# Ten of the last sixteen output blocks of an encoder layer: row scale on ScalarE, addition and store on GpSimd

## The chip, the core and the metric

The kernel runs on one core of a Trainium2 chip. The metric is the device time of one execution in microseconds (us), lower is better. The core has five engines with instruction queues of their own: TensorE (PE in the profile: matmuls; PEld: its weight loads), VectorE (DVE), ScalarE (ACT), GpSimd (POOL) and SyncE (SP, which here only issues DMA transfers). Each engine takes its instructions strictly in the order of its queue and waits on semaphores for the others.

## The reference

One encoder layer over 1024 tokens of width 2048. What matters here is its end: the merged branch output is multiplied with `w_out`, each row of the product is normalised by its own root mean square, multiplied with a gain and a gate per column, and added to the input.

```python
def rmsnorm(x, g):
    xf = x.astype(jnp.float32)
    xf = xf * lax.rsqrt(jnp.mean(xf * xf, axis=-1, keepdims=True) + EPS)
    return xf.astype(x.dtype) * g
...
    merged = g_a * (y_a @ w_br_attn) + g_p * (y_p @ w_br_pool)
    o = merged @ w_out
    return x + gate[:, None] * rmsnorm(o, post_g)
```

## The kernel before

All large products are done as Strassen products of 2 x 2 blocks, seven instead of eight. Each float32 operand is split into a rounded part and a remainder (`whi`, `wlo` for weights, `mh`, `ml` for the moving operand): ScalarE writes the rounded part (L95), VectorE the remainder (L96), and three matmuls (L1194 to L1196) multiply them.

The product with `w_out` is the last stage. The 1024 rows are eight row tiles T = 0 to 7 of 128 rows; the 2048 columns are four column blocks n = 0 to 3 of 512. `out_pair(half, i, ...)` runs four times, for (0, 0), (0, 1), (1, 0), (1, 1); a half is four row tiles, and i chooses two of the four column blocks. Each call runs seven products in the order A11, S3, S2, A12, A22, S1, S4 with six PSUM banks: `bx`, `bz` and `bv`, two of each, one for each of two row tiles. Bank `bz` is used on: after S1, ScalarE copies it out (`u4`, the two L1276 instructions `u<-Z`), and S4 then adds to it. So the matmuls of S4 on a bank wait for that copy.

As each block of `o` gets ready, `result` (L1279) takes the sum of squares of its 512 columns on ScalarE (`square`, L1204: an activation and a read of its accumulator) and multiplies the block with gain and gate on VectorE (L1284). When a row tile has all four blocks, `row_scale` (L1206) makes the factor of its 128 rows: a sum on VectorE, a square root on ScalarE, a reciprocal on VectorE. Then `finish_block` (L1213) does, per block, one VectorE instruction `r * scale + x` (L1215) and a store of 256 KB, which SyncE issues, except for the blocks of the first half, whose stores GpSimd issues.

The very end is the call (1, 1), `final`. Before its last product, S4, the blocks of T = 4 and 5 are complete: `after()`, which is `third_block` (L1415), finishes these eight. Then S4 runs 24 matmuls for the bank of T = 6, block 1 of that row tile gets ready, and its four blocks are finished; then 24 matmuls for T = 7 and the same again. The eight weight pieces of S4 have buffers of their own, and their splitting on ScalarE and VectorE (the last `whi` and `wlo`) stands in the queues around the finishing blocks. The order within each queue comes from a scheduler that places instructions by its own estimate; `keep` marks an instruction that is to stay in program order. The rows of `x` for T = 4 to 7 (`xr`) were loaded during earlier products.

Of the kernel before, what the change touches and what calls it, by code (L numbers as in the profile page):

```python
# [14 lines left out]
AF = mybir.ActivationFunctionType  # L15
ALU = mybir.AluOpType
# [26 lines left out]
def encoder_layer(ctx: ExitStack, tc: tile.TileContext, x, c, table, w_ada, b_ada, pre_g,  # L43
# [15 lines left out]
    nc = tc.nc  # L59
# [30 lines left out]
    def keep(ins):  # L90

        tc.keep_in_program_order(ins)
# [259 lines left out]
    for r0, src in ((0, c[0]), (16, b_ada[0, 0:D]), (32, b_ada[0, D:2 * D]),  # L352
                    (48, pre_g[0]), (64, b_merge[0]), (96, pool_scale[0])):
        n = src.shape[0] // P
# [421 lines left out]
    held = {}  # L776
# [414 lines left out]
    def out_mm(pb, op, name, j, t, w, first, last):  # L1191
        ts_ = slice(t * P, (t + 1) * P)
        hi, lo = (o_[:, j % 2, ts_] for o_ in op[name][j // 2])
        nc.tensor.matmul(pb, hi, w[0], start=first, stop=False, skip_group_check=True)  # L1194
        nc.tensor.matmul(pb, lo, w[0], start=False, stop=False, skip_group_check=True)  # L1195
        nc.tensor.matmul(pb, hi, w[1], start=False, stop=last, skip_group_check=True)  # L1196

    xrow, held = {}, {}

    def rows_of(T, n):  # L1200
        return out[T * P:(T + 1) * P, n * 512:(n + 1) * 512]
# [4 lines left out]
    def row_scale(T):  # L1206
        s_ = const.tile([P, 3], F32, tag="st", name=uid("st"), bufs=4)
        nc.vector.tensor_reduce(s_[:, 0:1], ssq[:, T], op=ALU.add, axis=AX.X)
        nc.scalar.activation(s_[:, 1:2], s_[:, 0:1], AF.Sqrt, bias=eps_t, scale=1.0 / D)
        nc.vector.reciprocal(s_[:, 2:3], s_[:, 1:2])  # L1210
        return s_[:, 2:3]

    def finish_block(T, n, scale, store=store):  # L1213
        r = held.pop((T, n))
        keep(nc.vector.scalar_tensor_tensor(r, r, scale, xrow.pop((T, n)), op0=ALU.mult, op1=ALU.add))  # L1215
        store(rows_of(T, n), r)

    def fetch_x_block(T, n, tile_of):
        xrow[T, n] = tile_of("xr")
        load(xrow[T, n], x[T * P:(T + 1) * P, n * 512:(n + 1) * 512])  # L1220
# [7 lines left out]
    def out_pair(half, i, op, between, after=None):  # L1228
# [50 lines left out]
        def result(blk, t, src, dst):  # L1279

            T, nh = half * 4 + (int(blk[1]) - 1) * 2 + t, int(blk[0]) - 1
            n = 2 * nh + i
            square(src, T, n)
            nc.vector.tensor_tensor(dst, src, g[nh], ALU.mult)  # L1284
            if stays:
                held[T, n] = dst
            else:
                nc.gpsimd.dma_start(o_d[T * P:(T + 1) * P, n * 512:(n + 1) * 512], dst)
# [41 lines left out]
        for t in range(2):  # L1330
            for j, w in enumerate(ws):
                out_mm(bz[t], op, "B22", j, t, w, False, j == len(ws) - 1)
            result("12", t, bz[t], c12[t])
            scale = row_scale(6 + t)
            for n in (0, 2, 3, 1):
                finish_block(6 + t, n, scale)

    nextm, nextt2 = [], {}
    scales = {}
# [4 lines left out]
    def first_rows(T, n):  # L1344

        def place(name):
            ring.rotate(-1)
            return ring[-1]

        def fetch():  # L1350
            if (T, n) not in held:
                held[T, n] = place("fo")
                keep(load(held[T, n], o_d[T * P:(T + 1) * P, n * 512:(n + 1) * 512]))
            fetch_x_block(T, n, place)

        def put_out():
            if T not in scales:
                scales[T] = row_scale(T)
            finish_block(T, n, scales[T], nc.gpsimd.dma_start)

        return fetch, put_out
# [45 lines left out]
    def between_11(n, jp):  # L1407
        if jp % 2 and n < 3:
            steps(1)
        if jp == JP - 1 and n in (2, 4):  # L1410
            for T in (4, 5) if n == 2 else (6, 7):
                for b in range(4):
                    fetch_x_block(T, b, lambda name: slot(name, F32))

    def third_block():  # L1415
        assert not side
        for T in (4, 5):
            scale = row_scale(T)
            for b in range(4):
                finish_block(T, b, scale)  # L1420

    out_pair(0, 0, ops[0], between_00)
    out_pair(0, 1, ops[0], between_01)
    out_pair(1, 0, ops[1], between_10)
    out_pair(1, 1, ops[1], between_11, third_block)


# [36 lines left out]
```

## Time and profile before

| | us |
|---|---|
| median of 3 runs | 2125.08 (2124.27 to 2125.27) |
| profiled execution, its own time | 2122.46 |
| span of its profile | 2120.7 |
| PE busy | 2089.0 (99%) |
| DVE busy | 1538.7 (73%) |
| ACT busy | 1109.5 (52%) |
| POOL busy | 20.4 (1%), 90 instructions |

The span runs from the first to the last recorded event of the execution; its own time is 1.8 us longer. The profile numbers times from the start of the span. "Busy" counts the time in which an engine had an instruction under way, and successive instructions of an engine overlap: four `whi` splits recorded with about 0.6 us each take 2.23 us together. So what one more instruction costs its queue is the distance from start to start, not the recorded length. DMA issues are not counted as busy. Landing is the time from an issue to the arrival of the last byte.

### The profile page before, as it was taken

Reading aid. Unit: us, or ns where it says so; the run is one execution under the profiler, and the core shown is the slowest. Engines: PE = TensorE matmul, PEld = TensorE weight load, DVE = VectorE, ACT = ScalarE, POOL = GpSimd, SP = SyncE. Lnnn points to the kernel's source line nnn. Section 1 sums busy time; section 2 is a strip of 40 time slices with the busy share of each in tenths; the row PEclk is TensorE's granted clock in tenths of the full one; section 3 lists DMA queues with packets and bytes.
Section 4 is the critical chain, followed back from the end, with each engine's and each line's share of the span. In section 5 each row is a group of like instructions: output and inputs, shape, how many; then the busy total and the mean of one; then the engine's idle time right before and its main releaser. Section 6 shows DMA issues by size and latency. Waiting matters only on the chain.

```text
span 2120.7 us, 28959 instructions
## 1 busy us (share of the span) xinstructions
PE 2089.0 (99%) x9567; PEld 1715.1 (81%) x9567; DVE 1538.7 (73%) x2754; ACT 1109.5 (52%) x2102; POOL 20.4 (1%) x90
## 2 busy tenths in 40 slices
PE   6999999999999999999999999999999999999998
PEld 4588888888888888888888888888788788888886
DVE  5786667777547676677777678856957977889667
ACT  5654444444474544666665544333645644767654
POOL 0000000000000000000000000000000000000000
PEclk9999999999999999999999999999999999999999
DMA  9886566899676356544645477676754556686996
GB/s 330 271 269 216 187 208 219 307 310 316 223 228 210 120 176 204 174 157 159 196 149 162 154 236 235 206 221 195 237 173 160 187 194 198 218 311 216 296 342 221
DMA packets 301718, 466.10 MB, mean 220 GB/s; under 512 B 23882, under 2 KB 144866, under 8 KB 301568
## 3 DMA queue, kind: packets, MB, share of 16 engines
q1 hardware_dynamic: 298192, 455.72, 65.9%
q0 software_dynamic: 3040, 8.48, 1.1%
q8 instruction: 75, 1.23, 0.2%
q14 instruction: 75, 0.61, 0.1%
q10 hardware_dynamic: 336, 0.06, 0.0%
HBM read 340.41 MB, written 125.85 MB: 220 GB/s over the span
## 4 chain that ended last, share of the span: by engine, by line
PE 90%; DVE 5%; DMA 3%; issue 1%; ACT 1%; SPq 0%; ACTq 0%; DVEq 0%
PE Z L235 30%; PE X L235 20%; PE V L235 20%; PE Z L1194 2%; PE Z L1195 2%; PE Z L1196 2%; PE V L1196 1%; PE X L1196 1%; PE X L1195 1%; PE V L1195 1%; PE V L1194 1%; PE X L1194 1%; PE GEMV L455 1%; DMA raw<-in_w_merge_dram 1%; DVE wlo L96 1%; PE PT L905 1%
## 5 line engine op out<-in xcount | busy, mean ns | idle before, releaser
L95 ACT ACTIVATE whi<-raw 128x512 fp32r<-128x512 f32 (+1 forms) x528 | 321.8, 610 | 526.1 <-PE Z L235 260.4
L96 DVE TENSOR_TENSOR wlo<-raw,whi 128x512 fp32r<-128x512 f32 (+1 forms) x528 | 347.0, 661 | 166.7 <-PE Z L235 129.8
L96 DVE TENSOR_TENSOR wlo<-wr,whi 128x512 fp32r<-128x512 f32 x224 | 151.0, 688 | 55.9 <-ACT whi L95 49.8
L95 ACT ACTIVATE whi<-wr 128x512 fp32r<-128x512 f32 x224 | 138.8, 629 | 89.7 <-DVE wlo L96 37.2
L102 DVE TENSOR_TENSOR raw<-raw,raw 128x512 f32<-128x512 f32 x80 | 55.2, 690 | 105.0 <-DMA raw<-in_w_merge_dram 77.2
L235 PE MATMUL V<-T3h,whi 128*128 128x512 f32 x336 | 92.0, 393 | 0.6 <-DVE u L102 0.6
L235 PE MATMUL X<-B11h,whi 128*128 128x512 f32 x336 | 92.0, 392 | 0.0
L95 ACT ACTIVATE whi<-ws 128x512 fp32r<-128x512 f32 (+1 forms) x88 | 53.7, 611 | 73.0 <-PE X L235 67.7
L235 PE MATMUL V<-T4l,whi 128*128 128x512 f32 x336 | 91.2, 390 | 0.7 <-DVE T4l L96 0.6
L235 PE MATMUL Z<-T1h,whi 128*128 128x512 f32 x336 | 91.6, 391 | 0.0
L235 PE MATMUL Z<-T2h,whi 128*128 128x512 f32 x336 | 91.5, 392 | 0.1
L235 PE MATMUL Z<-B22h,whi 128*128 128x512 f32 x336 | 91.5, 392 | 0.0
L235 PE MATMUL Z<-T2h,wlo 128*128 128x512 f32 x336 | 90.8, 390 | 0.5 <-DVE wlo L96 0.5
L235 PE MATMUL X<-B21h,whi 128*128 128x512 f32 x336 | 91.2, 391 | 0.0
L235 PE MATMUL V<-T4h,whi 128*128 128x512 f32 x336 | 91.2, 391 | 0.0
L235 PE MATMUL Z<-T1l,whi 128*128 128x512 f32 x336 | 91.0, 390 | 0.1
L235 PE MATMUL X<-B11l,whi 128*128 128x512 f32 x336 | 90.9, 390 | 0.0
L235 PE MATMUL X<-B11h,wlo 128*128 128x512 f32 x336 | 90.7, 390 | 0.0
L235 PE MATMUL Z<-B22l,whi 128*128 128x512 f32 x336 | 90.7, 390 | 0.0
L235 PE MATMUL V<-T3l,whi 128*128 128x512 f32 x336 | 90.7, 390 | 0.0
L235 PE MATMUL Z<-T1h,wlo 128*128 128x512 f32 x336 | 90.6, 390 | 0.0
L235 PE MATMUL X<-B21l,whi 128*128 128x512 f32 x336 | 90.6, 389 | 0.0
(315 smaller groups left out, 4819.3 us busy)
## 6 DMA issues: line engine op xcount, KB each, us to landing
part<-part_d SPq DMA_DIRECT2D x136, 256.0 KB, 4.8
ada<-in_w_ada_dram SPq DMA_DIRECT2D x128, 256.0 KB, 5.3
raw<-in_w_in_dram SPq DMA_DIRECT2D x64, 512.0 KB, 4.1
raw<-in_w_merge_dram SPq DMA_DIRECT2D x64, 512.0 KB, 5.8
wr<-ws_dS SPq DMA_DIRECT2D x64, 512.0 KB, 5.2
wr<-in_w_out_dram SPq DMA_DIRECT2D x48, 512.0 KB, 5.4
proj_d<-part SPq DMA_DIRECT2D x68, 256.0 KB, 2.2
sw<-in_w_out_dram SPq DMA_DIRECT2D x64, 256.0 KB, 5.7
```

The source lines that it names most:

```text
L95: ins = (nc.scalar.activation(hi, src, AF.Copy), nc.vector.tensor_tensor(lo, src, f32(hi), ALU.subtract))
L96: nc.vector.tensor_tensor(lo, src, f32(hi), ALU.subtract))
L102: return (eng or nc.vector).tensor_tensor(o, a, b, ALU.add)
L235: nc.tensor.matmul(ps, w_[:, i], op[mov][j][m_], start=fresh and i == 0 and n == 0, stop=i == nj - 1 and n == 2, skip_group_check=True)
L455: ins = nc.tensor.matmul(pv[g:g + 32, :], scz[:, kc, :], tile_of(kc), start=kc < 4, stop=kc >= 12, tile_position=(0, g))
L905: nc.tensor.transpose(pt[:, i * P:(i + 1) * P], p[:, i * P:(i + 1) * P], ident)
L1194: nc.tensor.matmul(pb, hi, w[0], start=first, stop=False, skip_group_check=True)
L1195: nc.tensor.matmul(pb, lo, w[0], start=False, stop=False, skip_group_check=True)
L1196: nc.tensor.matmul(pb, hi, w[1], start=False, stop=last, skip_group_check=True)
```

## The change

`finish_aside` is a second way to finish a block: ScalarE multiplies the block with the row scale (a Copy activation with a scale for each partition), GpSimd adds x, and GpSimd issues the store. All eight blocks of T = 4 and 5 take it, and block 0 of T = 6 and of T = 7. The other six blocks of T = 6 and 7 keep the VectorE instruction and the SyncE store.

```diff
+    def finish_aside(T, n, scale):
+        r = held.pop((T, n))
+        keep(nc.scalar.activation(r, r, AF.Copy, scale=scale))
+        keep(nc.gpsimd.tensor_tensor(r, r, xrow.pop((T, n)), ALU.add))
+        nc.gpsimd.dma_start(rows_of(T, n), r)
...
             for n in (0, 2, 3, 1):
-                finish_block(6 + t, n, scale)
+                (finish_aside if n == 0 else finish_block)(6 + t, n, scale)
...
             for b in range(4):
-                finish_block(T, b, scale)
+                finish_aside(T, b, scale)
```

Lines behind L1216 move down by six: L1276 and L1284 of before are L1282 and L1290 of the changed kernel.

ScalarE's queue, from the splitting of the last weight pieces (`whi`) to the two copies `u<-Z` that free the banks for S4. Before:

```order
L95 ACTIVATE whi_19955<-wr_19949 128x512
L95 ACTIVATE whi_19961<-wr_19959 128x512
L95 ACTIVATE whi_19965<-wr_19959 128x512
L1276 ACTIVATE u_4231_19969<-Z_19341 128x512
L1276 ACTIVATE u_4232_19970<-Z_19342 128x512
L95 ACTIVATE whi_19975<-wr_19973 128x512
```

And of the changed kernel, where `mo`, `c` and `u` with `st` are the blocks of T = 4 and their scale:

```order
L95 ACTIVATE whi_19955<-wr_19949 128x512
L1220 ACTIVATE mo_19009<-mo_19009,st_19991 128x512
L95 ACTIVATE whi_19961<-wr_19959 128x512
L1220 ACTIVATE c_4162_19731<-c_4162_19731,st_19991 128x512
L95 ACTIVATE whi_19965<-wr_19959 128x512
L1220 ACTIVATE mo_18912<-mo_18912,st_19991 128x512
L1282 ACTIVATE u_4231_19969<-Z_19341 128x512
L1220 ACTIVATE u_4140_19639<-u_4140_19639,st_19991 128x512
L1282 ACTIVATE u_4232_19970<-Z_19342 128x512
L95 ACTIVATE whi_19975<-wr_19973 128x512
```

Three scalings now stand ahead of the first copy `u<-Z` and a fourth ahead of the second. The four scalings of T = 5 stand further down, ahead of the square of T = 6.

VectorE's queue, from the last weight remainder (`wlo`) to the first finishing instruction of T = 6. Before:

```order
L96 TENSOR_TENSOR wlo_19980<-wr_19973,whi_19979 128x512
L1284 TENSOR_TENSOR p_4111_19532<-p_4111_19532,pg_19435 128x512
L1215 TENSOR_SCALAR u_4140_19639<-u_4140_19639,st_19991,xr_19629 128x512
L1215 TENSOR_SCALAR mo_19009<-mo_19009,st_20003,xr_19631 128x512
L1215 TENSOR_SCALAR c_4163_19732<-c_4163_19732,st_20003,xr_19633 128x512
L1215 TENSOR_SCALAR mo_18912<-mo_18912,st_20003,xr_19635 128x512
L1215 TENSOR_SCALAR u_4141_19640<-u_4141_19640,st_20003,xr_19637 128x512
L1284 TENSOR_TENSOR c_4242_20015<-Z_19341,pg_19433 128x512
L1208 TENSOR_REDUCE st_20044<-ssq_o 128x1
L1210 RECIPROCAL st_20044<-st_20044 128x1
L1215 TENSOR_SCALAR mo_19332<-mo_19332,st_20044,xr_19827 128x512
```

And of the changed kernel:

```order
L96 TENSOR_TENSOR wlo_19980<-wr_19973,whi_19979 128x512
L1290 TENSOR_TENSOR p_4111_19532<-p_4111_19532,pg_19435 128x512
L1290 TENSOR_TENSOR c_4242_20023<-Z_19341,pg_19433 128x512
L1208 TENSOR_REDUCE st_20052<-ssq_o 128x1
L1210 RECIPROCAL st_20052<-st_20052 128x1
L1215 TENSOR_SCALAR mo_18807<-mo_18807,st_20052,xr_19831 128x512
```

The finishing instructions of T = 4 and 5 are gone (three more of them stood further up, between weight remainders), and T = 6 has three instead of four; T = 7 likewise.

GpSimd's queue, whose last entries before were the stores of the first half. The changed kernel goes on behind them (the first of ten such pairs; those of T = 6 and 7 come last):

```order
L1216 DMA out_dram<-mo_18696 128x512
L1221 TENSOR_TENSOR mo_19009<-mo_19009,xr_19623 128x512
L1222 DMA out_dram<-mo_19009 128x512
L1221 TENSOR_TENSOR c_4162_19731<-c_4162_19731,xr_19625 128x512
L1222 DMA out_dram<-c_4162_19731 128x512
L1221 TENSOR_TENSOR mo_18912<-mo_18912,xr_19627 128x512
L1222 DMA out_dram<-mo_18912 128x512
```

Each store waits for the addition ahead of it, and each addition for a scaling on ScalarE. All ten pairs stand in one queue. SyncE's queue loses the ten stores and keeps six.

## Prediction

> **What bounds the kernel now.** The page first: PE is busy over the whole span except its two ends.
>
> ```profile
> span 2120.7 us, 28959 instructions
> PE   6999999999999999999999999999999999999998
> ```
>
> Nothing before the last product moves, so only the last 25 us count. I read the timeline of each engine there, beginning with PE and ACT around the copies that free the banks.
>
> ```profile
> 2100.78 0.50 PE L1194 MATMUL Z<-whi,mh 128*128 128x512 f32 x1
> ...
> 2111.57 0.39 PE L1196 MATMUL Z<-wlo,mh 128*128 128x512 f32 x1
> ...
> 2100.78 0.19 PEld L1194 LDWEIGHTS Z<-whi,mh 128*128 128x128 f32 x1 [0.35 <-ACT u L1276]
> ```
>
> ```profile
> 2094.48 2.23 ACT L95 ACTIVATE whi<-wr 128x512 fp32r<-128x512 f32 x4
> 2097.59 0.62 ACT L95 ACTIVATE whi<-wr 128x512 fp32r<-128x512 f32 x1
> 2099.09 1.15 ACT L95 ACTIVATE whi<-wr 128x512 fp32r<-128x512 f32 x2 [0.88 <-DMA wr<-ws_dS]
> 2100.15 0.58 ACT L1276 ACTIVATE u<-Z 128x512 f32<-128x512 f32 x1
> ...
> 2112.05 0.58 ACT L1204 ACTIVATE junk<-Z 128x512 f32<-128x512 f32 x1 [1.71 <-PE Z L1196]
> 2112.54 0.19 ACT L1204 ACTIVATION_READ_ACCUMULATOR junk<-Z 128x1 f32 x1
> 2114.01 0.29 ACT L1209 ACTIVATE st<-st,eps_t 128x1 f32<-128x1 f32 x1 [1.27 <-DVE st L1208]
> ```
>
> S4 cannot start until `u<-Z` has run: PE stands still for 0.35 us and starts at 2100.78, 0.63 after the copy's start. From there its 48 matmuls run without a gap; the last starts at 2111.57 and ends at 2111.96. The copy itself starts as soon as ACT has done the splits ahead of it. So ACT's queue up to 2100.15 is on the path, with 0.88 us of slack ahead of 2099.09 (it waits for a load there) and none behind.
>
> Then the end, in the chain of waits (start, length, what) and SP's last issue.
>
> ```profile
> 2112.65 0.66 DVE c L1215
> 2113.31 0.60 DVE c L1284
> 2113.91 0.07 DVE st L1208
> 2113.99 0.02 issue
> 2114.01 0.30 ACT st L1209
> 2114.32 0.02 issue
> 2114.34 0.17 DVE st L1210
> 2114.51 0.03 issue
> 2114.54 0.75 DVE mo L1215
> ...
> 2116.61 0.66 DVE c L1215
> ```
>
> ```profile
> 2113.23 0.68 DVE L1284 TENSOR_TENSOR c<-Z,pg 128x512 f32<-128x512 f32 x1
> 2116.53 0.74 DVE L1215 SCALAR_TENSOR_TENSOR c<-c,st,xr 128x512 f32<-128x512 f32 x1
> 2117.30 0.33 SPq L1216 DMA_DIRECT2D out_dram<-c  x1
> ```
>
> VectorE is behind: its gain multiply of T = 7 (L1284) could start when the square's accumulator is read, 2112.54 + 0.19 = 2112.73, and starts at 2113.23, because finishing blocks of T = 6 stand ahead. Then come sum, root, reciprocal, four finishing instructions 0.66 apart, and the last store.
>
> ```profile
> out_dram<-mo SPq DMA_DIRECT2D x8, 256.0 KB, 2.4
> out_dram<-mo POOLq DMA_DIRECT2D x1, 256.0 KB, 3.6
> DMA to landing us min/median/max: 3.6/5.7/7.6
> ```
>
> A store by SP in this stretch lands in 2.4 us (first row, median of eight from 2095 to 2121): 2117.30 + 2.4 = 2119.7, and the span ends 1.0 us later. GpSimd's eight `mo` stores from 2015 to 2062, where loads were dense, took 3.6 to 7.6 us (third row); the 3.6 is the second row, one store at 2021.
>
> **The change part by part.**
>
> *ScalarE and the banks.* From the four splits of 2.23 us, less one length of 0.62, three distances are 1.61, so one ACT instruction of this size takes 0.54 us of the queue. The first scaling fits into the 0.88 us gap: the reciprocals that it needs end at about 2098.57. The second and third stand between the splits and ahead of the first copy, where nothing idles: 2 x 0.54 = 1.08, with a few hundredths for the first, **1.1 us**. The copy starts at 2101.25 and PE at 2101.88. The fourth scaling delays only the second copy, needed 24 matmuls later. The last weight pieces come later too, but by the same 1.1 us or less, since VectorE has lost the finishing instructions between them. So PE ends at 2111.96 + 1.1 = 2113.06. Bounds: 0.6, if a scaling takes half that distance, to 1.7, if a third fails to fit the gap.
>
> *VectorE.* Ten finishing instructions go. Those of T = 4 and 5 buy only what VectorE was late by, 2113.23 - 2112.73 = 0.50; of T = 7's four one goes, 0.66. So the SP side ends at +1.1 - 0.50 - 0.66 = **-0.1 us**: the same as before. Whatever GpSimd does, the time can hardly fall.
>
> *GpSimd, one addition.* The trace has no addition on POOL. The nearest rows:
>
> ```profile
> L1452 POOL MEMSET const-float32-0.0<- 128x1 f32 x1 | 0.1, 98 | 0.2 <-issue 0.2
> masks.py:197 POOL MEMSET ident<- 128x128 f32 x1 | 0.2, 204 | 0.3 <-POOLq L1452 0.3
> masks.py:199 POOL TENSOR_SCALAR_AFFINE_SELECT ident<-ident 128x128 f32<-128x128 f32 x1 | 0.3, 282 | 0.0
> ```
>
> A write alone costs (204 - 98) / 127 = 0.83 ns an element, a read and a write (282 - 98) / 127 = 1.45, so a read 0.62. Two reads and a write are 2.07 ns, for 512 elements with the fixed 98 ns **1.16 us**. Bounds: 0.84 (as with one input) and 1.58 (each input at the full 1.45).
>
> *GpSimd, one store.* The closest two issues in its queue stand 0.66 apart:
>
> ```profile
> 1969.61 0.54 POOL L1216 DMA_DIRECT2D out_dram<-u  x1 [3.25 <-DVE u L1215]
> 1970.27 0.54 POOL L1216 DMA_DIRECT2D out_dram<-c  x1
> ```
>
> With 0.10 for the wait between addition and store (an estimate from the 0.12 between these two rows), a block costs 1.16 + 0.10 + 0.66 = 1.92 us of POOL's queue, if nothing disturbs it. The first scaling ends near 2099.2, T = 5's follow by 2107, and POOL never runs dry. So the tenth addition starts at 2099.2 + 9 x 1.92 = 2116.5, though its own scaling is done by 2115.75 (the T = 7 chain above, 1.1 - 0.50 later, plus 0.62). It is the **backlog** that decides. Its store is issued at 2116.5 + 1.26 = 2117.7. For landing I take 3.6, the row with the lightest traffic and the nearest to the quiet end; bounds 2.4 (as SP's) and 5.7. With 1.0 to the end: 2122.3, **+1.6**.
>
> [...]
>
> *GpSimd beside VectorE.* From 2099 to 2117 VectorE still runs 15 instructions with two inputs in SBUF: five `wlo`, four on `p`, six finishing.
>
> ```profile
> L96 DVE TENSOR_TENSOR wlo<-wr,whi 128x512 fp32r<-128x512 f32 x5 | 3.4, 682 | 0.0
> L1284 DVE TENSOR_TENSOR p<-p,pg 128x512 f32<-128x512 f32 x2 | 1.4, 682 | 0.0
> L102 DVE TENSOR_TENSOR p<-p,u 128x512 f32<-128x512 f32 x2 | 1.3, 682 | 0.0
> ```
>
> Nine at 0.60 and six at 0.66 from start to start are 9.4 us. Additions fill 1.16 / 1.92 = 60% of POOL's queue, so 5.7 us of VectorE's work falls beside one. Whether they slow each other no row shows; POOL's store issues keep at 0.54 beside a VectorE busy most of the time, but they read no tile. Bounds: nothing, and the whole 5.7. I take half, **2.8 us**, about 0.3 per block, because two-input work on both sides is just what the trace has not had.
>
> **Sum.** 2120.7 + 1.6 + 2.8 = 2125.1, +4.4. The profiled execution took 2122.46, 2.6 below the median of the runs; I move the median by the same: 2125.08 + 4.4 = **2129.5 us**.
>
> **The rivals.**
>
> *POOL undisturbed.* No slowing: +1.6, 2126.7. For it: 0.54 for every store. Against it: those rows are no additions.
>
> *POOL locked out.* An addition and a two-input VectorE instruction exclude each other, and VectorE goes first: the whole 5.7, +7.3; with an addition at 1.4, halfway to the upper bound, ten times 0.24 more, +9.7. Middle 2133.6. [...]
>
> *Not slower.* The addition costs 0.84, as with one input, so a block takes 1.60 and the tenth addition starts when its scaling ends, 2115.8; and its store lands in 2.4 as SP's do: 2115.8 + 0.94 + 2.4 + 1.0 = 2120.1, so SP's side ends last at -0.1: 2125.0. It decides below 1.84 us a block and about 2.9 us of landing, together. Against it: both are at their bounds.
>
> *The relief does not come.* VectorE or PE is stalled by weight pieces split late on top of the rest: +6 or more.
>
> **How the numbers follow.** Chances: forecast 0.40 (+2.7 to +6.5), undisturbed 0.27, locked out 0.22, not slower 0.06, last 0.05. What a measurement of this kernel can tell from no change is 0.2%, 4.25 us. Above it: a bit more than half of the forecast's 0.40, and 0.22 and 0.05, together 0.52. Faster by that much would need a sum that none of these gives: 0.02. Within: 0.46. The range runs from 2125.5, under the undisturbed case, to 2135.5, past the locked-out one.
>
> **What would show it.** In the changed kernel's profile: PE's wait for `u<-Z` grown from 0.35 to about 1.4 us and its last matmul near 2112.7; VectorE idle between T = 6 and T = 7, and its last finishing instruction near 2116.5; ten POOL pairs from 2099 without idle time, 1.9 to 2.4 us apart, ending near 2121; the last landing POOL's and no longer SP's. I am wrong if POOL sits idle ahead of its last addition, if its additions are far from 1.2 to 1.5 us from start to issue, or if a PE gap other than that one opens.

## The result: 9 us slower, and the profile after

The changed kernel takes 2132.68 us (median of six runs, 2131.26 to 2133.74), the kernel before 2123.49 in six runs (2122.42 to 2125.27): a ratio of 1.0042, 95% interval 1.0031 to 1.0053, so 9 us slower. The profiled execution took 2131.3 us with a span of 2129.5, 8.8 above the span before.

TensorE first, since it set the time before: the timeline of PE in the changed kernel (start, length, operation; in brackets the idle time ahead and its releaser), from the last matmul of S1.

```profile
2099.66 0.39 PE L1196 MATMUL Z<-wlo,mh 128*128 128x512 f32 x1
2100.81 0.50 PE L1194 MATMUL Z<-whi,mh 128*128 128x512 f32 x1 [0.76 <-ACT u L1282]
...
2105.27 0.39 PE L1195 MATMUL Z<-whi,ml 128*128 128x512 f32 x1
2106.65 0.50 PE L1196 MATMUL Z<-wlo,mh 128*128 128x512 f32 x1 [0.99 <-DVE wlo L96]
...
2107.21 0.40 PE L1195 MATMUL Z<-whi,ml 128*128 128x512 f32 x1
2110.95 0.79 PE L1196 MATMUL Z<-wlo,mh 128*128 128x512 f32 x1 [3.34 <-DVE wlo L96]
2111.54 0.63 PE L1194 MATMUL Z<-whi,mh 128*128 128x512 f32 x1
2111.97 0.63 PE L1195 MATMUL Z<-whi,ml 128*128 128x512 f32 x1
...
2119.09 0.39 PE L1196 MATMUL Z<-wlo,mh 128*128 128x512 f32 x1
```

In the kernel before, that last matmul of S1 stands here:

```profile
2100.46 0.39 PE L1196 MATMUL Z<-wlo,mh 128*128 128x512 f32 x1
```

The stage that ran without a gap before now stops twice, both times for a weight remainder (`wlo`) that VectorE has not written, and behind the second stop the matmuls start 0.43 us apart instead of 0.23. The windows show the same (length, busy time and count of PE, PEld, DVE, ACT and POOL, then the granted TensorE clock, DMA share, GB/s):

```profile
2106.20:2109.60 3.40, 0.96 (x3) 0.48 (x3) 3.40 (x3) 1.43 (x3) 2.93 (x4) 1.00 0.20 77
2109.60:2116.40 6.80, 5.45 (x13) 4.29 (x14) 6.41 (x7) 1.70 (x4) 5.85 (x7) 0.50 0.36 135
2116.40:2119.80 3.40, 3.08 (x14) 2.18 (x12) 1.66 (x2) 0.23 (x1) 0.99 (x2) 1.00 0.77 288
```

From 2109.6 to 2116.4, TensorE was granted half its clock (0.50); full clock (1.00) stands on both sides.

Why the remainders are late shows where VectorE and GpSimd are laid side by side. VectorE's timeline:

```profile
2100.79 3.63 DVE L102 TENSOR_TENSOR p<-p,u 128x512 f32<-128x512 f32 x2 [0.26 <-ACT u L1282]
2104.35 2.25 DVE L96 TENSOR_TENSOR wlo<-wr,whi 128x512 fp32r<-128x512 f32 x1
...
2108.67 2.22 DVE L96 TENSOR_TENSOR wlo<-wr,whi 128x512 fp32r<-128x512 f32 x1
2110.82 2.24 DVE L1290 TENSOR_TENSOR p<-p,pg 128x512 f32<-128x512 f32 x1
2112.98 0.68 DVE L1290 TENSOR_TENSOR c<-Z,pg 128x512 f32<-128x512 f32 x1
...
2120.29 0.69 DVE L1290 TENSOR_TENSOR c<-Z,pg 128x512 f32<-128x512 f32 x1 [2.24 <-ACT junk L1204]
...
2122.94 1.75 DVE L1215 SCALAR_TENSOR_TENSOR c<-c,st,xr 128x512 f32<-128x512 f32 x1
```

And GpSimd's:

```profile
2098.09 1.29 POOL L1221 TENSOR_TENSOR mo<-mo,xr 128x512 f32<-128x512 f32 x1 [44.14 <-ACT mo L1220]
...
2104.74 1.29 POOL L1221 TENSOR_TENSOR u<-u,xr 128x512 f32<-128x512 f32 x1
...
2106.91 1.28 POOL L1221 TENSOR_TENSOR mo<-mo,xr 128x512 f32<-128x512 f32 x1
...
2115.54 1.29 POOL L1221 TENSOR_TENSOR mo<-mo,xr 128x512 f32<-128x512 f32 x1
...
2122.42 1.72 POOL L1221 TENSOR_TENSOR mo<-mo,xr 128x512 f32<-128x512 f32 x1 [4.73 <-ACT mo L1220]
```

Before the change, a VectorE instruction with two inputs in SBUF took 0.68 us, and the next one started 0.60 after it:

```profile
2104.15 0.68 DVE L1284 TENSOR_TENSOR p<-p,pg 128x512 f32<-128x512 f32 x1
2104.75 0.68 DVE L96 TENSOR_TENSOR wlo<-wr,whi 128x512 fp32r<-128x512 f32 x1
```

Now six of them, from 2100.79 to 2112.98, take 12.2 us from start to start, 2.03 each instead of 0.60. Each ends about 0.56 us after the addition beside it: the addition at 2104.74 ends at 2106.03, the remainder at 2106.60. So VectorE gets through one instruction per pair of addition and store (2.17 us). The product with one input in PSUM (`c<-Z`, 2112.98) keeps its 0.68, but it runs mostly beside a store issue, so the trials below decide about it. The additions stay at 1.27 to 1.31, one at 1.42. VectorE loses all of it, GpSimd next to nothing, except at the very end, where the tenth addition and VectorE's last instruction slow each other (1.72 for 1.29, and 1.75 for 0.74).

GpSimd is idle for 4.73 us ahead of its tenth addition, so its backlog does not set the end. The chain of waits hides that: it follows POOL's queue back, and that time stands in it as 4.93 us of "issue" from 2117.44.

The 8.8 us by stages, from the starts of matmuls here and in the timeline of before: up to the last S1 matmul **-0.80** (2099.66 for 2100.46; 0.7 of it is there when the product with `w_out` begins, 1827.5 for 1828.2, far ahead of the change, so this is scatter between executions); bank copy **+0.83** (S4's first matmul 1.15 behind that, for 0.32); S4 from first to last matmul **+7.49** (18.28 for 10.79); from the last matmul to the end of the span **+1.28** (10.41 for 9.13). S4's share is the first stop, 1.38 - 0.23 = 1.15, the second, 3.74 - 0.23 = 3.51, and the lower clock: the 13 intervals from 2110.95 to 2116.55 take 5.60 rather than 2.95, 2.65 more; 0.2 remain.

### The profile page after: what moved, and what is told of

It is laid out like the page before. It is cut to its first block, busy times and chain, and to the rows that moved or that the text cites. A ratio compares the mean times of both kernels' runs of the same rounds, so it can differ in the third digit from the quotient of the medians.

```text
span 2129.5 us, 28982 instructions
## 1 busy us (share of the span) xinstructions
PE 2092.7 (98%) x9567; PEld 1716.8 (81%) x9567; DVE 1545.2 (73%) x2744; ACT 1115.2 (52%) x2112; POOL 39.5 (2%) x110
## 4 chain that ended last, share of the span: by engine, by line
PE 91%; DVE 3%; DMA 2%; issue 1%; POOL 1%; SPq 0%; ACT 0%; ACTq 0%; POOLq 0%; DVEq 0%
PE Z L235 30%; PE V L235 20%; PE X L235 20%; PE Z L1194 2%; PE Z L1195 2%; PE Z L1196 2%; PE V L1194 1%; PE X L1194 1%; PE V L1195 1%; PE X L1195 1%; PE X L1196 1%; PE V L1196 1%; PE GEMV L455 1%; PE PT L905 1%; PE XT L407 1%
```

## The experiments

Three parts of the change could make the remainders late: the additions (theory A: an addition on GpSimd keeps VectorE's two-input instructions out), the scalings (theory B: ScalarE writes `whi` later), the store issues (theory C). The first four runs take them apart, on one chip, with 25 runs of the kernel before (median 2123.19).

**The scaling alone.** ScalarE scales, VectorE adds, SyncE stores:

```diff
+        keep(nc.scalar.activation(r, r, AF.Copy, scale=scale))
+        keep(nc.vector.tensor_tensor(r, r, xrow.pop((T, n)), ALU.add))
+        store(rows_of(T, n), r)
```

> The scalings stay on ScalarE in the changed kernel's order; the additions go to VectorE and the stores to SyncE. Theory A (a GpSimd addition keeps two-input VectorE work out while it runs, so the last weight remainders come late, PE waits and its clock drops): the wait at the bank copy stays at about 1.2 us (0.8 more than before), the two waits for wlo (1.4 and 3.8 us) vanish, the clock stays at 1.00, and the time is +0.3 to +1.0 us against before. Theory B (eight scalings in ScalarE's queue make the weight pieces late): the waits for wlo stay at 3 us or more and the time at +5 us or more.

Measured: 2125.42, ratio 1.0008 (0.9999 to 1.0017): 2.2 us by the medians, more than I expected, but not clear of no change. PE waits for the bank copy, 1.1 us, and for no remainder; VectorE's instructions keep 0.68, the last remainder among them:

```profile
2106.75 0.68 DVE L96 TENSOR_TENSOR wlo<-wr,whi 128x512 fp32r<-128x512 f32 x1
```

All ten scalings stand in ScalarE's queue, and the remainders are in time: theory B falls.

**The store alone.** VectorE's one instruction as before, GpSimd issues the ten stores:

```diff
+        keep(nc.vector.scalar_tensor_tensor(r, r, scale, xrow.pop((T, n)), op0=ALU.mult, op1=ALU.add))
+        nc.gpsimd.dma_start(rows_of(T, n), r)
```

> All finishing work on VectorE as before; only the ten stores are issued by GpSimd. Theory A: nothing is locked, VectorE's instructions keep 0.66 and 0.74 us, PE has only its 0.35 us wait, and the time is 0 to +1 us, since the last landing is still one of SyncE's. Theory C (GpSimd's store issues disturb VectorE): VectorE instructions beside the issues stretch beyond 1 us and the time is +4 us or more.

Measured: 2124.28, ratio 1.0004 (0.9995 to 1.0013). The issues take 0.54 us, and VectorE's instructions beside them 0.69 and 0.75 (GpSimd, then VectorE):

```profile
2102.50 0.54 POOL L1221 DMA_DIRECT2D out_dram<-mo  x1 [45.31 <-DVE mo L1220]
2102.72 0.75 DVE L1220 SCALAR_TENSOR_TENSOR c<-c,st,xr 128x512 f32<-128x512 f32 x1
```

Theory C falls: the issues by themselves hold nothing up. PE's wait for the bank copy was not the 0.35 that I expected but 0.89, with no scaling in ScalarE's queue: ScalarE waits 0.92 us for the load of a weight piece ahead of the copy.

**The addition with SyncE's store.**

```diff
-        nc.gpsimd.dma_start(rows_of(T, n), r)
+        store(rows_of(T, n), r)
```

> Scaling on ScalarE and addition on GpSimd as in the changed kernel, but SyncE stores. Theory A: the gaps that GpSimd's store issues leave between additions (0.87 us) shrink to 0.3 us or less while scalings are at hand, so VectorE is kept out for the four additions of T = 4 together and again for those of T = 5; the waits of PE for wlo stay, 3 to 6 us in sum, and the time is +5 to +10 us. The additions of T = 4 and 5 end by about 2112 instead of 2115. Theory C: without the store issues no VectorE instruction stretches, and the time is +1 us or less.

Measured: 2128.19, ratio 1.0023 (1.0014 to 1.0033). Scalings and additions together, without a store issue between the additions, give about half of the loss, 5.0 us, and 2.8 more than the scalings alone. The timeline of VectorE there, and then GpSimd's:

```profile
2107.26 0.68 DVE L96 TENSOR_TENSOR wlo<-wr,whi 128x512 fp32r<-128x512 f32 x1
...
2115.41 1.75 DVE L1215 SCALAR_TENSOR_TENSOR c<-c,st,xr 128x512 f32<-128x512 f32 x1
2117.08 0.68 DVE L1290 TENSOR_TENSOR c<-Z,pg 128x512 f32<-128x512 f32 x1
```

```profile
2103.34 1.75 POOL L1221 TENSOR_TENSOR mo<-mo,xr 128x512 f32<-128x512 f32 x1
2105.04 1.75 POOL L1221 TENSOR_TENSOR u<-u,xr 128x512 f32<-128x512 f32 x1
2108.79 1.50 POOL L1221 TENSOR_TENSOR mo<-mo,xr 128x512 f32<-128x512 f32 x1 [2.00 <-DMA out_dram<-u]
```

The two engines take turns, one instruction of each per 1.70 us, and both pay. The waits for remainders are smaller than expected (weight loads 0.41 and 0.67 late, PE's idle time 0.24 in all, clock at 1.00): from 2106.8 to 2108.8 GpSimd is idle (the profile names a transfer as the releaser, but the scaling that the next addition needs ends only at 2108.71), and the last two remainders (2107.26 and 2108.47) start in that pause. More is lost behind S4: T = 7's gain multiply starts at 2117.08, because T = 6's finishing instructions ahead of it are stretched. That the additions cost is confirmed; my size for the waits was not.

**One input on GpSimd.** Scaling and store as in the change, but GpSimd multiplies the block by 1.0 in place of the addition of x:

```diff
-        keep(nc.gpsimd.tensor_tensor(r, r, xrow.pop((T, n)), ALU.add))
+        keep(nc.gpsimd.tensor_scalar(r, r, 1.0, None, op0=ALU.mult))
```

> As the changed kernel, but GpSimd multiplies the block by 1.0 in place of the addition, so the ten blocks leave out x. If any GpSimd instruction that reads SBUF locks out two-input VectorE work: VectorE instructions beside it stretch to 0.7 plus its length (0.8 to 0.9 us), PE waits for wlo 0.5 to 3 us in sum, and the time is +2 to +6 us. If only GpSimd's second input does it: no stretch, only the longer bank wait, and the time is 0 to +1.5 us.

Measured: 2133.32, ratio 1.0048 (1.0033 to 1.0063), as slow as the change, for another reason. VectorE's two-input instructions take 0.68 to 1.10, one at the very end 1.30, and PE waits for no remainder; S4 starts 2.10 us behind the last matmul of S1 and goes on without a stop. But the multiplication with one input (1.50 us) is longer than the addition with two (1.27 to 1.31 in the change), as GpSimd's timeline shows:

```profile
2126.03 1.50 POOL L1222 TENSOR_SCALAR mo<-mo 128x512 f32<-128x512 f32 x1
```

Ten pairs, all but one 2.43 us apart, without idle time from 2103.71 on, in a run in which the first scaling also came late: here it is the backlog that decides. The time alone would have read as "the second input does not matter"; the views say that it does.

**Side by side, by itself.** Behind the end of the kernel before, five trials on scratch tiles, in each five instructions of VectorE or ScalarE against five of GpSimd:

```diff
+    both_sides(lambda: nc.vector.tensor_tensor(z[2], z[2], z[3], ALU.add), pool_two)
+    both_sides(lambda: nc.vector.tensor_tensor(z[2], zp, z[3], ALU.add), pool_two)
+    both_sides(lambda: nc.vector.tensor_scalar(z[2], z[2], 0.5, None, op0=ALU.mult), pool_two)
+    both_sides(lambda: nc.scalar.activation(z[2], z[2], AF.Copy), pool_two)
+    both_sides(lambda: nc.vector.tensor_tensor(z[2], z[2], z[3], ALU.add), pool_one)
```

> The kernel before with five short trials at its end on scratch tiles, 128x512 each: five instructions on GpSimd beside five on another engine. (1) GpSimd additions beside VectorE additions of two SBUF inputs: theory A wants both stretched, a VectorE one to 1.7 to 2.2 us and one per addition. (2) beside VectorE additions with one input in PSUM, (3) beside VectorE multiplications of one SBUF input, (4) beside ScalarE copies: theory A in its narrow form (only a second SBUF input of VectorE collides) wants 0.6 to 0.8 us in all three; in its wide form (any VectorE instruction is kept out) (2) and (3) stretch to 1.5 us or more. (5) one-input GpSimd multiplications beside VectorE additions of two SBUF inputs: 0.7 to 1.1 us on VectorE, as in the run with one input.

The groups of that stretch (busy time, mean ns of one, idle time; `zp` lies in PSUM, all else in SBUF):

```profile
L1443 POOL TENSOR_TENSOR z<-z,z 128x512 f32<-128x512 f32 x20 | 27.3, 1367 | 66.5 <-DVE z L1430 65.0
L1446 POOL TENSOR_SCALAR z<-z 128x512 f32<-128x512 f32 x5 | 8.3, 1656 | 0.4
L1448 DVE TENSOR_TENSOR z<-z,z 128x512 f32<-128x512 f32 x5 | 7.2, 1442 | 0.1
L1450 DVE TENSOR_SCALAR z<-z 128x512 f32<-128x512 f32 x5 | 5.9, 1180 | 0.4 <-POOL z L1440 0.3
L1452 DVE TENSOR_TENSOR z<-z,z 128x512 f32<-128x512 f32 x5 | 4.0, 807 | 0.4 <-POOL z L1440 0.3
L1449 DVE TENSOR_TENSOR z<-zp,z 128x512 f32<-128x512 f32 x5 | 3.5, 691 | 0.4 <-POOL z L1440 0.3
L1451 ACT ACTIVATE z<-z 128x512 f32<-128x512 f32 x5 | 3.1, 630 | 25.6 <-POOL z L1440 25.5
```

L1448 is the case of the change: both inputs in SBUF beside additions, 1442 ns in the mean (the first, ahead of any addition, 682; the median 1632). GpSimd's five additions there take 8.21 us from first start to last end, for 6.63 beside L1449, so both engines pay. With one input of VectorE's addition in PSUM (L1449) it is 691: for an addition, it is the second SBUF input that counts. But a VectorE multiplication with a single SBUF input (L1450) is held up too, though its first took 427: median 1368, between what the two forms of the theory wanted. No run here shows why. ScalarE (L1451) shows no delay: its five take 629 to 631 ns each, 3.28 us together, and eight such copies without GpSimd, in the run with a late piece below, 5.27, so 0.66 from start to start in both. Beside a GpSimd instruction with one input (L1452) VectorE loses little, 807 in the mean, and GpSimd is the one that goes up, to 1656 in the mean, for the 1.50 us above. So theory A holds, and for more than two-input work: of what was tried, what goes free beside an addition is VectorE reading one of its inputs from PSUM, and ScalarE.

**All scalings behind the last remainder.** The change, with the scales of T = 4 and 5 made from a read of the last remainder, so that no addition can start beside one:

```diff
+            first = row_scale(T)
+            nc.vector.scalar_tensor_tensor(scale, f32(last_lo)[:, 0:1], 0.0, first, op0=ALU.mult, op1=ALU.add)
```

> As the changed kernel, with the scalings of T = 4 and 5 held behind the last weight remainder by the same tiny instruction. Theory A: PE has no wait for wlo and its clock stays at 1.00; what then decides is GpSimd's queue: ten pairs 2.16 us apart from about 2105.6, the tenth addition starts near 2125 without idle time ahead of it, and the time is +8 to +11 us. If the queue did not matter, the time would be within +2 us.

Measured: 2135.56 beside 2122.29, ratio 1.0063 (1.0046 to 1.0080), some 13 us slower and 2 more than the upper end of what I expected. The same ten additions, later: PE stops for no remainder, S4 takes 10.77 from first to last matmul, the clock stays at 1.00. The price is the queue of GpSimd, and the finishing of T = 6 (VectorE, then GpSimd):

```profile
2113.66 2.21 DVE L1215 SCALAR_TENSOR_TENSOR mo<-mo,st,xr 128x512 f32<-128x512 f32 x1
...
2120.09 0.68 DVE L1290 TENSOR_TENSOR c<-Z,pg 128x512 f32<-128x512 f32 x1
```

```profile
2107.49 1.29 POOL L1221 TENSOR_TENSOR mo<-mo,xr 128x512 f32<-128x512 f32 x1 [51.35 <-ACT mo L1220]
...
2126.94 1.27 POOL L1221 TENSOR_TENSOR mo<-mo,xr 128x512 f32<-128x512 f32 x1
```

From 2107.49 to 2126.94 GpSimd never idles, 2.16 us a pair, and the backlog decides. Here, where the additions start nine microseconds later than in the change, the backlog is what the prediction took it for.

**Half of them, behind.** T = 4 on VectorE as before; T = 5 aside, behind the last remainder; block 0 of T = 6 and 7 aside:

```diff
+            if T == 4:
+                for b in range(4):
+                    finish_block(T, b, first)
+                continue
```

> The four blocks of T = 4 are back on VectorE, those of T = 5 and block 0 of T = 6 and 7 go aside, and the scalings of T = 5 take their scale through a tiny VectorE instruction that also reads the last weight remainder, so that no addition starts before it is done. Theory A: no wait of PE for wlo, the bank wait as before, clock 1.00; GpSimd's six pairs, 2.2 us apart from about 2106.5, end near 2119, and VectorE's finishing instructions of T = 6 and 7 stretch to 1.3 to 2.2 us beside the additions: the time is +1.5 to +4 us. If the remainders were late for another reason than the additions, the waits for wlo stay above 2 us and the time is +5 us or more.

Measured: 2128.72 beside 2122.29, ratio 1.0028 (1.0018 to 1.0038), 6 us slower where I expected at most 4. PE waits for no remainder, but six additions are enough to hold up T = 6's finishing instructions on VectorE:

```profile
2114.13 1.81 DVE L1215 SCALAR_TENSOR_TENSOR p<-p,st,xr 128x512 f32<-128x512 f32 x1
2115.86 2.23 DVE L1215 SCALAR_TENSOR_TENSOR c<-c,st,xr 128x512 f32<-128x512 f32 x1
2118.02 0.68 DVE L1290 TENSOR_TENSOR c<-Z,pg 128x512 f32<-128x512 f32 x1
```

T = 7's gain multiply could start at 2114.85, when its square's accumulator is read, and starts 3.2 us later. The hold-up moves to the next place with two-input work.

**The clock: a late piece in the kernel before.** Is the half clock a consequence of PE's stop, or of what GpSimd and VectorE do there? Ten ScalarE copies of the last S4 weight piece onto itself, ahead of its rounding:

```diff
+                if not ring and jp == JP - 1:
+                    for _ in range(10):
+                        keep(nc.scalar.activation(raw[:, 1], raw[:, 1], AF.Copy))
```

> The kernel before, with ten Copy activations of the last weight piece onto itself ahead of its split, about 5.4 us of ScalarE; GpSimd does nothing at the end. The last two weight pieces are then ready about 4 us late, so PE stands still for 3.5 to 4.5 us in one go. If PE's clock falls after any such stop: the granted clock reads 0.5 for about 5 us behind it, matmuls start 0.43 us apart instead of 0.23, and some 2.5 us are lost on top of the stop. If the fall came from GpSimd's or VectorE's state in the changed kernel: the clock stays at 1.00 and only the stop is lost.

Measured: 2125.27 beside 2122.29, clock at 1.00. Not a test: the scheduler put matmuls of T = 7 ahead of the late piece, and PE stopped for about 1.1 us only. So the run was repeated with eight and with fourteen copies, and the 48 matmuls of S4 held in their order:

```diff
-                    for _ in range(10):
+                    for _ in range(8):
...
-                out_mm(bz[t], op, "B22", j, t, w, False, j == len(ws) - 1)
+                out_mm(bz[t], op, "B22", j, t, w, False, j == len(ws) - 1, keep)
```

> The kernel before, with eight ScalarE copies of the last S4 weight piece onto itself ahead of its rounding, and S4's 48 matmuls held in the order that the kernel before has, so that TensorE meets the late piece in one stop; nothing of the change is in it. From the copies' 0.66 us start to start and the first S4 matmul at 2100.72 in the run with ten unpinned copies, the stop should be one of about 3.6 us, as long as the second one of the changed kernel (3.74 between two matmuls). If such a stop alone lowers the clock: matmuls behind it 0.43 apart for about 5 us, PEclk near 0.5 in that window, S4 from first to last matmul about 10.8 + 3.5 + 2.5 = 16.8 us. Rival, the slow matmuls of the changed kernel come from something that GpSimd or VectorE do there: matmuls stay 0.23 apart, PEclk 1.00, S4 about 14.3 us.

> As the run with eight copies, with fourteen: one stop of about 7.6 us. If a stop alone lowers the clock, it does so here too, matmuls 0.43 apart behind it for about 5 us (about 2.5 us on top of the stop), and if the shorter stop of the other run did not lower it, the threshold lies between the two. Rival: clock stays 1.00 and S4 takes about 10.8 + 7.4 = 18.2 us from first to last matmul; then what lowered the clock in the changed kernel lies in GpSimd's or VectorE's work.

Measured: 2130.63 and 2137.25 beside 2122.70, one execution each. Both traces are already 2 to 3 us behind that of before when the product with `w_out` begins near 1830, far ahead of the copies, so I read S4 alone. PE with eight copies, from the stop to the last matmul, and its windows:

```profile
2107.69 0.39 PE L1196 MATMUL Z<-wlo,mh 128*128 128x512 f32 x1
2111.62 0.50 PE L1194 MATMUL Z<-whi,mh 128*128 128x512 f32 x1 [3.54 <-ACT whi L95]
...
2120.21 0.39 PE L1196 MATMUL Z<-wlo,mh 128*128 128x512 f32 x1
```

```profile
2109.60:2113.00 3.40, 1.38 (x5) 0.83 (x6) 2.13 (x4) 2.42 (x5) 0.00 (x0) 1.00 0.65 231
2113.00:2116.40 3.40, 3.40 (x10) 2.67 (x9) 1.33 (x4) 0.98 (x3) 0.00 (x0) 0.50 0.00 0
2116.40:2119.80 3.40, 3.40 (x17) 2.80 (x16) 2.34 (x4) 0.00 (x0) 0.00 (x0) 1.00 0.67 240
```

And the windows with fourteen:

```profile
2109.70:2113.10 3.40, 0.00 (x0) 0.00 (x0) 2.47 (x4) 3.24 (x6) 0.00 (x0) 1.00 0.68 252
2113.10:2123.30 10.20, 5.98 (x14) 4.73 (x15) 3.19 (x7) 5.51 (x11) 0.00 (x0) 0.50 0.07 25
```

GpSimd does nothing there, and VectorE's instructions are those of the kernel before, at their old lengths: the stop brings the half clock without them. With eight copies, S4 takes 2120.21 - 2103.82 = 16.39 us from first to last matmul, expected 16.8: 10.79 of before, 3.70 for the stop, 1.90 for the restart and the clock (1.60 in the nine intervals at half clock). With fourteen it takes 22.00, 8.23 of it for the stop and 2.98 for the clock. The half clock (0.50) lasted 3.4 us with eight copies, 6.8 in the changed kernel and 10.2 with fourteen. In the 3.40 us ahead of it PE was busy for 1.38 us with eight copies, for 0.96 in the changed kernel and for none with fourteen. What sets its length, and the delay from the stop to its start, no run here shows.

No variant with additions on GpSimd was faster than the kernel before, and the two without them (scaling alone, store alone) cannot be told from it.

## Why the prediction was right, and where it failed

The direction was right and the time lay inside the range, but the change was twice the forecast: +9.2 by the medians, against +4.4. The forecast reached its sign by a wrong step, and that the time lay in the range is luck in good part: the backlog that the sum rests on did not set the end, and 7.3 us of two stops and a lower clock, which the sum does not have, came in its place.

- **Bank copy.** Forecast +1.1, and the two traces differ by 0.83. That looks like the term, but it is not shown to be: from the last matmul of S1 to the first of S4 it is 1.15 to 2.10 us in the four traces with scalings ahead of the copy, and 0.23 to 1.38 in those without, where a late load of a weight piece held ScalarE as well (0.92 us with the store alone). The trace of before, with 0.32, is at the low end.
- **One addition.** Estimated at 1.16 us from the fill and the select at the program's start, measured 1.27 to 1.29. Addition and store, with the 0.30 that the store waits behind the addition, take 2.17 us of the queue; forecast 1.92 undisturbed.
- **Landing of GpSimd's stores.** Taken as 3.6 us from a row in a stretch dense with loads, measured 2.6, as this row of the transfers from 2095 on shows (the last number is the median landing):

```profile
out_dram<-mo POOLq DMA_DIRECT2D x6, 256.0 KB, 2.6
```

- **The backlog.** "POOL never runs dry", so that it decides. It did run dry, for 4.73 us ahead of its last addition, because T = 7 had become so late that the backlog was gone by then. That was one sign that I had named for being wrong; a gap of PE other than the one for `u<-Z` was another, and it came too.
- **GpSimd beside VectorE: the step that failed.** The prediction had 5.7 us of VectorE's work beside additions, took half of it as a slowing, and put that on GpSimd's queue; the sharpest rival, too, had VectorE go first. In the run GpSimd kept its 1.29 us and VectorE was held: six instructions, 12.2 us for 3.6, 8.6 lost. The sentence that fell with it is that the last weight pieces come later "by the same 1.1 us or less, since VectorE has lost the finishing instructions between them". The instructions were gone, but those that stayed took three times as long, two remainders came late, and PE stopped for 1.15 and 3.51 us.
- **The clock.** 2.65 us were not in any of the cases. A stop of PE was priced at its own length only.
- **The rivals.** "Locked out" had the exclusion that the runs then showed (a VectorE addition of 0.68 us took 1.63 beside additions), with the wrong engine as its loser. "The relief does not come" (+6 or more, chance 0.05) is what happened: PE stalled by late weight pieces, though they were late on VectorE's side.
- **VectorE at the end.** The relief came nearly as forecast, 0.46 for 0.50, and one instruction less: T = 7's gain multiply starts 0.72 us behind the square's start (2120.29 for 2119.57), before 1.18, and T = 7 has three finishing instructions. But the last of them is stretched to 1.75 beside the tenth addition, and end and landing lie 1.28 us further from the last matmul than before.

What is shown: the additions, and neither scalings nor store issues by themselves, hold VectorE up; the two stops of TensorE for a late piece, 3.93 and 8.46 us from start to start, were followed by a clock of 0.50 with no work of GpSimd beside them. What stays open: how much of the wait for the bank copy is the scalings', why a VectorE instruction that starts ahead of an addition, during the store issue (2104.35 and 2104.74), still ends behind it by the recorded starts, and why in the change GpSimd loses nothing, while without stores between the additions both pay.

## What to carry to other kernels

Moving elementwise work from VectorE to an idle GpSimd was no relief here, where both engines then read two inputs from SBUF at the same time: price it at what VectorE loses, here up to 1.57 us on one instruction for an addition that spared it 0.66. Ask of each engine that is slowed what it still has to deliver to TensorE in that stretch. The stops of TensorE from 3.7 us on were followed by half clock here, so that the price was their length and 1.9 to 3.0 us more.

## What the runs showed of the hardware that was not expected

- At 128 x 512 in float32, GpSimd's multiplication with one input (1.50 us) takes longer than its addition with two (1.29).
- An addition of GpSimd holds VectorE up to 2.2 us when stores are issued between additions, and 1.63 to 1.77 when additions follow each other; the store issues alone do not disturb VectorE (0.69 and 0.75 beside them). Starting first, by the recorded times, did not settle which of the two is held: in the trial by itself VectorE's first instruction starts 0.26 us ahead of the first addition and keeps its 0.68; in the change's rows the remainder at 2104.35 starts 0.39 us ahead of the addition at 2104.74 and ends 0.57 us behind it.
- From start to start, 1.1 to 2.1 us between two matmuls left the clock at 1.00; 3.7 to 8.5 us halved it for 3.4 to 10.2 us.
